# Token dispatch with weights on one Trainium2 core: later loads on the store queue, later products on VectorE alone

## The chip, the core and the metric

The kernel runs on one core of a Trainium2 chip. Three parts of the core matter here. VectorE (DVE in the profile) and ScalarE (ACT) multiply; 16 DMA engines move data between the device memory and the on-chip memory (SBUF, 128 partitions). A DMA is issued by an engine's instruction stream into a queue: those of SyncE (SP) go to queue q1 in this profile, those of ScalarE to queue q10. Both queues are served by the same 16 DMA engines.

The metric is the device time of one execution in microseconds (us), lower is better. The time before the change is the median of three runs.

## What is computed

Every token's 512 values are copied k = 2 times, each copy multiplied by its own weight. The indices are not used.

```python
# x: (16, 1024, 512) f32, expert_weights: (16, 1024, 2) f32
x_expanded = x[:, :, np.newaxis, :].repeat(k, axis=2)
weights = expert_weights[..., np.newaxis]
return (x_expanded * weights).astype(np.float32)     # (16, 1024, 2, 512)
```

So 33.5 MB are read and 67.1 MB are written, and there is one multiplication for each value written.

## The kernel before

The 16384 tokens are laid over 128 partitions, 128 tokens in each, and are worked on in six tiles: five of 24 tokens per partition and one of 8 (line 33). The text calls them tile 0 to tile 5. Each tile has these steps:

- **The load** of the tile's x into a buffer of the pool `x_pool`, which has two (line 79). L0 to L5 stand for the loads of tiles 0 to 5. A load of 24 tokens moves 6.29 MB (6144 KB, 48 KB in each partition); L5 moves a third of that. L0 is cut into six pieces (line 81), the others are one DMA each. Line 83 chooses the queue: SyncE for the last tile, ScalarE for all others.
- **The products**, in two halves of 12 tokens (`TO`), each into its own buffer `o_tile` of the pool `o_pool`, which also has two (line 98). In a half, VectorE takes tokens 0 to 3 and 6 to 9 of the 12 in two broadcast instructions of 4 tokens by 2 copies (line 121, 128 x 4096 values), and ScalarE takes tokens 4, 5, 10 and 11, one instruction for each token and copy (line 104, 128 x 512 values, eight in a half). The first half of tile 0 is different: it is made of single products on both engines (lines 104 and 110).
- **The stores**, one DMA for each half, issued on SyncE (line 137). S0a and S0b stand for the stores of tile 0, S1a and S1b for those of tile 1, and so on; tile 5 has one store, S5, of 8 tokens. A store of 12 tokens moves 6.29 MB, as much as a load of 24.

The order of issue is the program's order. `load(0)` and `load(1)` come before the loop; `load(i + 2)` comes at the end of iteration i (line 141), behind both stores of tile i. It writes the buffer that tile i was read from, so it waits until the products of tile i are done. The products of a half wait for the store that last read their `o_tile` buffer, which is the store two halves earlier, and for their tile's load. The framework derives all these waits from the buffers; each engine and each issuing stream works through its instructions in order. At the head, three small DMAs on SyncE bring the weights (lines 54 to 59).

Of the kernel before, what the change touches and what calls it, by code (L numbers as in the profile page):

```python
# [1 line left out]

# [4 lines left out]


@with_exitstack
def kernel(  # L10
    ctx: ExitStack,
    tc: tile.TileContext,
    x: bass.AP,
    expert_indices: bass.AP,
    expert_weights: bass.AP,
    out: bass.AP,
):
    nc = tc.nc

    batch, seq, hidden = x.shape  # L20
    k = expert_weights.shape[-1]
    P = nc.NUM_PARTITIONS
    ntok = batch * seq
    assert ntok % P == 0
    A_TOTAL = ntok // P

    f32 = mybir.dt.float32
    row = k * hidden
    TX = 24
    TO = 12  # L30
    CH = 4

    groups = [[24], [24], [24], [24], [24], [8]]
    assert sum(sum(g) for g in groups) == A_TOTAL

    xf = x.rearrange("b s h -> (b s) h")
    of = out.rearrange("b s k h -> (b s) (k h)")
    wf = expert_weights.rearrange("b s k -> (b s) k")

    w_pool = ctx.enter_context(tc.tile_pool(name="w_pool", bufs=1))  # L40
    x_pool = ctx.enter_context(tc.tile_pool(name="x_pool", bufs=2))
    o_pool = ctx.enter_context(tc.tile_pool(name="o_pool", bufs=2))

    w_tile = w_pool.tile([P, A_TOTAL * k], f32)

    def rows(of_all, done, T):
        return of_all[done * P : (done + T) * P, :].rearrange(
            "(p a) n -> p (a n)", a=T
        )

    T0 = sum(groups[0])
    G = len([g for g in groups[1:] if sum(g) == T0])
    head = (1 + G) * T0
    nc.sync.dma_start(out=w_tile[:, : T0 * k], in_=rows(wf, 0, T0))
    nc.sync.dma_start(
        out=w_tile[:, T0 * k : head * k].rearrange("p (g n) -> p g n", g=G),
        in_=wf[T0 * P : head * P, :].rearrange("(g p a) n -> p g (a n)", g=G, p=P),
    )
    nc.sync.dma_start(
        out=w_tile[:, head * k :], in_=rows(wf, head, A_TOTAL - head)  # L60
    )

    tiles = []
    done = 0
    for group in groups:
        T = sum(group)
        a0 = 0
        for n in group:
            tiles.append((done, T, a0, n))
            a0 += n  # L70
        done += T

    loaded = []

    def load(i):
        if i >= len(tiles):
            return
        done, T, a0, n = tiles[i]
        x_tile = x_pool.tile([P, TX * hidden], f32)
        src = rows(xf, done, T)  # L80
        step = TX // 6 if i == 0 else n

        queue = nc.sync if i == len(tiles) - 1 else nc.scalar
        for at in range(0, n, step):
            queue.dma_start(
                out=x_tile[:, at * hidden : (at + step) * hidden],
                in_=src[:, (a0 + at) * hidden : (a0 + at + step) * hidden],
            )
        loaded.append(x_tile)

    for i in range(2):
        load(i)
    for i, (done, T, a0, n) in enumerate(tiles):
        x_tile = loaded[i]
        outr = rows(of, done, T)
        for t in range(n):
            if t % TO == 0:
                o_tile = o_pool.tile([P, TO * row], f32)
            single = i == 0 and t < TO
            for kk in range(k if single or t % TO % 6 > 3 else 0):  # L100
                c = (done + a0 + t) * k + kk
                o = t % TO * row + kk * hidden
                if not single or c % 3 == 2:
                    nc.scalar.mul(  # L104
                        out=o_tile[:, o : o + hidden],
                        in_=x_tile[:, t * hidden : (t + 1) * hidden],
                        mul=w_tile[:, c : c + 1],
                    )
                    continue
                nc.vector.tensor_scalar(  # L110
                    out=o_tile[:, o : o + hidden],
                    in0=x_tile[:, t * hidden : (t + 1) * hidden],
                    scalar1=w_tile[:, c : c + 1],
                    scalar2=None,
                    op0=mybir.AluOpType.mult,
                )
            if not single and t % TO % 6 == 0:
                c = (done + a0 + t) * k
                o = t % TO * row
                m = min(CH, n - t)  # L120
                nc.vector.tensor_tensor(  # L121
                    out=o_tile[:, o : o + m * row].rearrange(
                        "p (t k h) -> p t k h", t=m, k=k
                    ),
                    in0=x_tile[:, t * hidden : (t + m) * hidden]
                    .rearrange("p (t h) -> p t h", t=m)
                    .unsqueeze(2)
                    .to_broadcast([P, m, k, hidden]),
                    in1=w_tile[:, c : c + m * k]
                    .rearrange("p (t k) -> p t k", t=m)  # L130
                    .unsqueeze(3)
                    .to_broadcast([P, m, k, hidden]),
                    op=mybir.AluOpType.mult,
                )
            if (t + 1) % TO == 0 or t + 1 == n:
                at = t // TO * TO
                nc.sync.dma_start(  # L137
                    out=outr[:, (a0 + at) * row : (a0 + t + 1) * row],
                    in_=o_tile[:, : (t + 1 - at) * row],
                )  # L140
        load(i + 2)

# [1 line left out]
_INS = ['x', 'expert_indices', 'expert_weights']  # L144
_OUTS = [((16, 1024, 2, 512), 'float32')]


# [23 lines left out]
```

## Time and profile before

| | |
|---|---|
| median of three runs | 240.34 us (240.26 to 242.69) |
| the profiled execution | 240.03 us |
| its span in the profile | 238.1 us |
| VectorE busy | 92.2 us (39%), 36 instructions |
| ScalarE busy | 54.2 us (23%), 85 instructions |
| queue q1 (SyncE: weights, stores, L5) | 69.34 MB, 67.5% of 16 DMA engines' span |
| queue q10 (ScalarE: L0 to L4) | 31.46 MB, 31.2% |

Span is the time from the first to the last event of the profile; what lies around it is 1.93 us here. The share of a queue is the time that its packets took on the DMA engines, so that 100% for both together would be 16 engines busy for the whole span. The profile also has the chain of waits that ended last, the instructions in order of time, and a table of stretches with the busy time of each engine, the share of the DMA engines and their GB/s.

Beside these views the trace holds a record of each DMA packet: its queue, start, duration and size. A load or store of 6.29 MB is 128 packets of 49152 bytes, one for each partition and eight on each DMA engine.

### The profile page before, as it was taken

The page shows a single profiled execution, that of the slowest core. Times are in us where ns is not written, and L with a number is a line of the kernel's source. Part 1 is how long each engine was busy: PE and PEld are TensorE (multiplying, and loading weights), DVE is VectorE, ACT ScalarE, POOL GpSimd, SP SyncE. Part 2 cuts the span into 40 slices and gives each one's busy share as a digit, 9 for nine tenths or more (in the row PEclk, how much of TensorE's full clock was granted, in tenths as well). Part 3 has the DMA queues.
Part 4 walks back from the last instruction along what each step waited for, and adds up shares of the span by engine and source line. Part 5 has one row for each costly group of instructions (what it writes and reads, how often), then busy time and mean ns, then how long its engine had stood idle before and what let it go on. Part 6 is the DMA issues. An engine that isn't in the chain of part 4 may idle for free.

```text
span 238.1 us, 232 instructions
## 1 busy us (share of the span) xinstructions
DVE 92.2 (39%) x36; ACT 54.2 (23%) x85; POOL 0.2 (0%) x4
## 2 busy tenths in 40 slices
DVE  0890240003919500391068085003919549019000
ACT  0841210003408000340061080003408044012000
POOL 0000000000000000000000000000000000000000
DMA  6998999999999999999999999999999999999996
GB/s 246 423 441 362 516 413 396 429 495 396 396 504 421 396 421 504 396 398 495 429 396 413 504 405 396 479 446 396 413 495 413 396 416 465 405 495 421 396 440 264
DMA packets 3986, 100.80 MB, mean 423 GB/s; under 512 B 1169, under 2 KB 1169, under 8 KB 1169
## 3 DMA queue, kind: packets, MB, share of 16 engines
q1 hardware_dynamic: 2544, 69.34, 67.5%
q10 hardware_dynamic: 1440, 31.46, 31.2%
q14 instruction: 2, 0.01, 0.0%
HBM read 33.69 MB, written 67.11 MB: 423 GB/s over the span
## 4 chain that ended last, share of the span: by engine, by line
DMA 62%; DVE 18%; another core or an unknown queue 10%; DVEq 1%; issue 0%; SPq 0%
DMA out_dram<-o_tile 50%; DVE o_tile L121 18%; DMA x_tile<-in_x_dram 12%; DVEq L166 1%; DVEq L121 0%; SPq L137 0%
## 5 line engine op out<-in xcount | busy, mean ns | idle before, releaser
L121 DVE TENSOR_TENSOR o_tile<-x_tile,w_tile 128x4096 f32<-128x4096 f32 (+1 forms) x20 | 85.6, 4316 | 121.0 <-DMA out_dram<-o_tile 85.7
L104 ACT ACTIVATE o_tile<-x_tile,w_tile 128x512 f32<-128x512 f32 x84 | 52.9, 709 | 155.0 <-DMA out_dram<-o_tile 115.8
L110 DVE TENSOR_SCALAR o_tile<-x_tile,w_tile 128x512 f32<-128x512 f32 x16 | 6.6, 483 | 6.6 <-DMA x_tile<-in_x_dram 6.6
L104 ACT ACT_TABLE_LOAD x1 | 1.3, 1283 | 6.6 <-DMA x_tile<-in_x_dram 6.6
L155 POOL MEMSET const-bfloat16-1.0<- 128x1 bf16 x1 | 0.1, 101 | 0.0
L155 POOL MEMSET const-uint8-127<- 128x1 uint8 x1 | 0.1, 101 | 0.0
L155 POOL MEMSET const-float32-0.0<- 128x1 f32 x1 | 0.1, 98 | 0.2 <-issue 0.2
L155 POOL MEMSET const-float32-1.0<- 128x1 f32 x1 | 0.1, 98 | 0.0
## 6 DMA issues: line engine op xcount, KB each, us to landing
out_dram<-o_tile SPq DMA_DIRECT2D x10, 6144.0 KB, 31.0
x_tile<-in_x_dram ACTq DMA_DIRECT2D x4, 6144.0 KB, 42.2
x_tile<-in_x_dram ACTq DMA_DIRECT2D x6, 1024.0 KB, 10.5
out_dram<-o_tile SPq DMA_DIRECT2D x1, 4096.0 KB, 17.4
x_tile<-in_x_dram SPq DMA_DIRECT2D x1, 2048.0 KB, 24.6
w_tile<-in_expert_weights_dram SPq DMA_DIRECT2D x1, 96.0 KB, 11.2
w_tile<-in_expert_weights_dram SPq DMA_DIRECT2D x1, 24.0 KB, 3.4
w_tile<-in_expert_weights_dram SPq DMA_DIRECT2D x1, 8.0 KB, 13.3
```

The source lines that it names most:

```text
L104: nc.scalar.mul(out=o_tile[:, o : o + hidden], in_=x_tile[:, t * hidden : (t + 1) * hidden], mul=w_tile[:, c : c + 1],)
L110: nc.vector.tensor_scalar(out=o_tile[:, o : o + hidden], in0=x_tile[:, t * hidden : (t + 1) * hidden], scalar1=w_tile[:, c : c + 1], scala ...
L121: nc.vector.tensor_tensor(out=o_tile[:, o : o + m * row].rearrange("p (t k h) -> p t k h", t=m, k=k), in0=x_tile[:, t * hidden : (t + m) * ...
L155: nc = _bacc.Bacc("TRN2", target_bir_lowering=False, num_devices=1)
L166: with _tile.TileContext(nc) as tc:
```

## The change

Two things change. First, every load from tile 2 on (L2 to L5) is issued on SyncE's stream, where it stands behind the second store of the tile two before it; L0 and L1 stay on ScalarE's. Second, from tile 2 on ScalarE makes no products: VectorE takes all 12 tokens of a half in three broadcast instructions of 4 tokens, at tokens 0, 4 and 8, and in tile 5 two instructions of 4 tokens. Tiles 0 and 1 are worked on as before (`shared`).

```diff
-        queue = nc.sync if i == len(tiles) - 1 else nc.scalar
+        queue = nc.sync if i >= 2 else nc.scalar
...
             single = i == 0 and t < TO
-            for kk in range(k if single or t % TO % 6 > 3 else 0):
+            shared = i < 2
+            step = 6 if shared else CH
+            for kk in range(k if single or shared and t % TO % 6 > 3 else 0):
                 c = (done + a0 + t) * k + kk
                 o = t % TO * row + kk * hidden
                 if not single or c % 3 == 2:
...
-            if not single and t % TO % 6 == 0:
+            if not single and t % TO % step == 0:
                 c = (done + a0 + t) * k
                 o = t % TO * row
                 m = min(CH, n - t)
```

## The prediction, made before the changed kernel ran

> **What bounds the kernel now.** I read the page's busy shares and DMA queues first, then the table of stretches, then the chain of waits with its order of time, and last the packet records. The page:
>
> ```profile
> DVE 92.2 (39%) x36; ACT 54.2 (23%) x85; POOL 0.2 (0%) x4
> ...
> DMA  6998999999999999999999999999999999999996
> ...
> q1 hardware_dynamic: 2544, 69.34, 67.5%
> q10 hardware_dynamic: 1440, 31.46, 31.2%
> ```
>
> The two queues together took 98.7% of 16 engines' span; neither multiplying engine is busy half of it. The table of stretches (length, busy time and count of each engine, clock, share of the DMA engines, GB/s) shows whether a stage hides a hole:
>
> ```profile
> 33.00:62.00 29.00, 4.57 (x2) 4.74 (x8) 0.00 (x0) 1.00 1.00 432
> 62.00:120.00 58.00, 21.72 (x5) 10.29 (x17) 0.00 (x0) 1.00 1.00 434
> 120.00:164.00 44.00, 17.52 (x4) 10.02 (x16) 0.00 (x0) 1.00 1.02 442
> 164.00:236.00 72.00, 32.91 (x8) 17.59 (x28) 0.00 (x0) 1.00 0.99 428
> ```
>
> There is none. By the packet records, 16 packets are in flight in every microsecond from 3 to 235; the first starts at 1.7 and the last ends at 236.9. Of 1792 packets of 49152 bytes, 1762 took exactly 1815 ns, loads and stores alike, with one queue active or two. So a 6.29 MB transfer costs 8 x 1.815 = 14.52 us of all engines, and the 100.66 MB of loads and stores cost 128 x 1.815 = 232.3 us in any order. The rest is 1.7 us at the head, 1.2 us behind the last packet, and 2.9 us more, of which some 2.1 us is small and overlapping packets in the first 20 us. The DMA engines are the bound. The chain of waits names stores and products, but each of its waits lies beside full DMA engines.
>
> **Part 1, L2, L3 and L4 from q10 to q1** (L5 is on q1 already). Nothing is added: three issues of 0.36 us leave ScalarE's stream for SyncE's, where issues of 0.33 to 0.82 us already lie between waits of up to 33.1 us. SyncE then waits for nothing new: a load needs the products that the store ahead of it has just waited for. S(i+1)a now stands behind the load's issue, and waits for its products far longer than that. The order of transfers does change. Before, a load shared the engines packet by packet with stores; now it follows S(i)b whole. What I must know is whether one queue alone keeps the engines full over the joints. The row is S3b, L5, S4a, all on q1 with q10 empty. The first engines end S3b at 192.49 us, L5 starts at 192.50; L5 ends from 197.55, S4a starts from 197.36. In the stretch from 180 to 200 the packets took 0.15 us per engine more than their bytes at 1815 ns per 49152. Three more loads with two such joints each cost 3 x 0.15 = 0.45 us at most; at the other end the loads' own excess on q10, 0.13 us from 20 to 140 us, is saved. I take +0.15, between the ends.
>
> **Part 2, products on VectorE alone.** From tile 2 on 52 ScalarE instructions go (16 in each of tiles 2, 3, 4 and 4 in tile 5) and VectorE's 13 of 4096 values and one of 2048 become 20 of 4096. The rows:
>
> ```profile
> L121 DVE TENSOR_TENSOR o_tile<-x_tile,w_tile 128x4096 f32<-128x4096 f32 x19 | 83.4, 4423 | 121.0 <-DMA out_dram<-o_tile 85.7 <-DMA x_tile<-in_x_dram 35.4
> L104 ACT ACTIVATE o_tile<-x_tile,w_tile 128x512 f32<-128x512 f32 x84 | 52.9, 709 | 155.0 <-DMA out_dram<-o_tile 115.8 <-DMA x_tile<-in_x_dram 39.1
> ```
>
> The broadcast took 4424 to 4426 ns whether or not ScalarE ran beside it. A pair with its issue took 8.83 us (179.16 to 187.99); three take 3 x 4.42 less two overlaps of some 0.08, with the issue 13.2. Each half becomes 4.4 us later; VectorE's total rises by 7 x 4.42 less 2.28 for the short one, 28.7: about 121 us of 238. None of it is on the path as long as each store is issued before its queue runs dry. That cover I now work out.
>
> **The queue after the change.** S2a starts at 120.0 and S3a at 163.5 before; by then the same transfers are done in both orders, so these times stand if no hole opens. Counting in steps of 14.52 us: S0b ends at 61.9, then L2 to 76.4, S1a to 91.0, S1b to 105.5, L3 to 120.0, S2a to 134.5, S2b to 149.0, L4 to 163.5, S3a to 178.0, S3b to 192.5, L5 to 197.4, S4a to 211.9, S4b to 226.4, S5. A landing reaches the products 1.3 us after the first engines end it (S3b 192.49, product at 193.83; S4a 211.86, product at 213.19), and 0.5 to 0.7 after the last one does; that is the row for q1 alone. Beside loads on q10 it took 2.2 us after the last end (S0b: 69.33, product at 71.53; S1a: 96.88, product at 99.07). The issue of each store, and its lead before its queue turn:
>
> - S1a at 66.3 as before (L1 is untouched), turn 76.4: lead 10. S1b: VectorE is free at 66.2, issue 75.0, turn 91.0: lead 16.
> - S2a: buffer free at 91.0 + 1.3, issue 105.5, turn 120.0: lead 14.5. S2b, S3a, S3b repeat this 14.5 us apart or so: leads 14.5.
> - S4a: 178.0 + 1.3 + 13.2 = 192.5, turn 197.4: lead 4.9. S4b: 192.5 + 1.3 + 13.2 = 207.0, turn 211.9: lead 4.9. S5: 211.9 + 1.3 + 8.8 = 222.0, turn 226.4: lead 4.4. Before, these were 9.4, 9.2 and 6.5:
>
> ```profile
> 187.99 25.07 DMA out_dram<-o_tile
> ...
> 213.19 4.43 DVE o_tile L121
> ```
>
> The short L5 and the end make the difference: between a half's buffer and its turn lie 14.5 us of another transfer and L5's 4.8, not 29, and for S5 14.5 alone. The loads land at 77.7, 121.3, 164.8 and 198.7, each some 14.5 us ahead of the products that need them.
>
> How much lead is needed? The lower bound is the first load: issued at 0.72, first packet at 1.81, so 1.1 us into idle engines. The upper bound is S3b: issued at 173.49, it started at 178.00 straight behind S3a, so 4.5 us was enough. Issues into busy engines showed their first packet after 3.9 (S0a) to 5.1 us (L3), but the engines were full meanwhile. Leads of 4.9, 4.9 and 4.4 thus cost nothing, or at the worst reading (5.1 needed) 0.2 for S4a and 0.7 for S5, 0.9 us; S4b adds none, since a late S4a moves its turn and not its products. I take 0, by S3b, the nearest row.
>
> A rule of the Trainium skill speaks against this cover: "DMA: Bandwidth & Descriptors", section "Anatomy of one DMA — SWDGE (gpsimd) path", gives a DMA some 2.0 us of fixed cost, mostly the receipt after the last byte. The 2.2 us beside q10 agree with it, the 0.5 us from S4a's last end (212.71) to its product (213.19) don't; by the rule the leads in the tail would be an estimated 1.5 us shorter.
>
> The sum: 238.1 + 0.15 + 0, so a span of some 238.3 and, with 1.93 around it, 240.2 for the profiled execution (240.03). The median stands 0.3 above that: 240.5.
>
> **The rivals.**
>
> - *Slower: the single queue stutters.* With q10 empty from 55 us on, a hole at a joint between load and store is filled by nothing. Six joints are new (S0b-L2, L2-S1a, S1b-L3, L3-S2a, S2b-L4, L4-S3a). At the 1.1 us of a start into idle engines they cost 6.6, so 247; it decides by 1% from 0.4 us a joint. Against it: S3b-L5-S4a without a hole. For it: L5's packets are of 16384 bytes, no 48 KB load has yet followed a store in one queue. 6%.
> - *Slower: the tail's stores come late.* If more lead is needed than there is, S4a and S5 leave the engines idle, each by the difference. With 5.85 us needed that is 0.95 + 1.45 = 2.4, the 1%; with 7 it is 2.1 + 2.6 = 4.7: 245. S3b's 4.5 without a hole is against it. 3%.
> - *Slower: late landings.* If stores in the tail reach the products 2.2 us behind their last end, as beside q10, and not 0.5, the leads of S4a and S5 fall by 1.7 to 3.2 and 2.7; against 4.5 needed that loses 1.3 + 1.8 = 3.1: 243.6. Every landing of the tail, where q10 was already empty before, is against it. 1%. The skill's rule above is of this kind.
> - *Faster: one kind of transfer at a time runs better.* Only the excess after 20 us, some 0.4 us, is there to win; more would need packets under 1815 ns, and the 128 packets of S2a, which ran alone, took that too. Over 1% would be 237.9 or less. 2%.
> - *It doesn't do what it says:* the framework could hold a load on SyncE for another transfer, with S(i+1)a behind it. L5's wait was 27 ns. A hold of up to one transfer passes beneath the leads of 14.5 us. No rival in time.
>
> **How the numbers follow.** Forecast, engines full throughout: 88%, 240.5, with the worst joints and leads 240.3 + 0.45 + 0.9 = 241.7; with all excess after 20 us saved 239.9. The runs of before spread from 240.26 to 242.69, so a median can stand a few tenths off: range 239.7 to 241.9. It leaves out the rivals, 12%, and little else. Within 1% (237.9 to 242.7), about what a measurement of this kernel can tell from no change: 88%; slower 6 + 3 + 1 = 10%; faster 2%.
>
> **What would show it.** Right: both queues' shares still sum to about 98.7%, with q10 at some 12.6 MB and q1 at 88.2; 1.00 in every stretch from 33 to 236; VectorE near 121 us, ScalarE near 21 us (52 x 0.63 less); S2a's, S4a's and S5's issues near 105, 192 and 222; loads that land some 15 us after the store ahead of them instead of sharing. Wrong at the joints: a share under 1 near 62, 105 and 149. Wrong in the tail: slices under 9 from 195 on. Packets that no longer take 1815 ns would overturn the whole sum.

## The result and the profile after

The changed kernel is slightly slower: 242.36 us (median of 20 runs, 240.54 to 243.23) against 240.36 us for the kernel before in the same series (20 runs, 239.88 to 243.5). The ratio is 1.0058, with a 95% interval of 1.0037 to 1.0079, or 1.4 us; it is made without disturbed runs and lies near the ratio of the means (242.10 against 240.72 without the slowest run of before). The plain medians are 2.0 apart because 14 of the 20 changed runs took 242.1 us or more and only 4 of the 20 before did. By the ratio the loss is within 1%, as forecast, but it is not zero.

The profiled execution took 241.27 us (before: 240.03), with a span of 239.1 us (238.1). So of its 1.24 us more, 1.0 lies in the span and 0.24 around it. The second part is steady: time less span was 2.14 to 2.23 us in all 20 runs of the changed kernel, and 1.88 to 1.97 in 29 runs of before. Its page answers the lines shown of before:

```profile
DVE 120.2 (50%) x42; ACT 21.5 (9%) x33; POOL 0.2 (0%) x4
...
DMA  6998999999999999999999999999999989999994
...
q1 hardware_dynamic: 2976, 88.21, 85.7%
q10 hardware_dynamic: 1008, 12.58, 12.8%
```

Both parts did what they say: VectorE has the work of ScalarE from tile 2 on, and q1 has all loads but L0 and L1. The two queues' shares sum to 98.5% (98.7% before). The table of stretches of the changed kernel (length, busy time and count of VectorE, ScalarE and GpSimd, clock, share of the DMA engines, GB/s), at the same places as before and with the first microsecond behind them:

```profile
33.00:62.00 29.00, 4.92 (x2) 4.95 (x8) 0.00 (x0) 1.00 1.00 432
62.00:120.00 58.00, 38.70 (x9) 5.08 (x9) 0.00 (x0) 1.00 1.00 432
120.00:164.00 44.00, 26.19 (x6) 0.00 (x0) 0.00 (x0) 1.00 1.02 439
164.00:236.00 72.00, 34.95 (x8) 0.00 (x0) 0.00 (x0) 1.00 1.00 430
236.00:237.00 1.00, 0.00 (x0) 0.00 (x0) 0.00 (x0) 1.00 0.16 66
```

The DMA engines are full up to 236 us, as before. There is no hole at the joints and none in front of the late stores. What is new is the last line. The table books a packet where it starts, and S5's packets of 32 KB take 1.21 us: a share of 0.16 in one microsecond is two packets that start after 236 us (2 x 1.21 / 16 = 0.15). Before, none did:

```profile
236.00:237.00 1.00, 0.00 (x0) 0.00 (x0) 0.00 (x0) 1.00 0.01 0
```

So two of the 16 engines still had a whole packet to start when others were about to end. The packet records say the same: the first engine ends its last packet at 236.04 us before and at 236.24 after, the last one at 236.90 before and 237.88 after. I call the difference of the two the **spread**: 0.86 us before, 1.64 after. Of the 0.98 us that the last packet moved, 0.78 is spread. Most of the loss in the span is not in the engines' mean work; it is in the one that comes last.

Where the spread grows can be read from each transfer's last packet on its first and its last engine (changed kernel, us, from the packet records):

```
S0b 0.49 | L2 0.49 | S1a 0.49 | S1b 0.49 | L3 0.69 | S2a 0.69 | S2b 0.69
L4 1.17 | S3a 1.17 | S3b 1.17 | L5 1.55 | S4a 1.76 | S5 1.63
```

No store from S1a to S3b changes it. L3, L4 and L5 do. (Before, the same row is 0.57 after S1b, 0.60 from S2b to S3b, 0.85 after L5, with L3 and L4 shared with stores.) L2 has three long packets too, up to 190 ns over 1815, and the spread stayed at 0.49.

### The profile page after: what moved, and what is told of

Same layout as the page of the kernel before. It is cut to its first block, busy times and chain, and to the rows that moved or that the text cites. A ratio compares the mean times of both kernels' runs of the same rounds, so it can differ in the third digit from the quotient of the medians.

```text
span 239.1 us, 173 instructions
## 1 busy us (share of the span) xinstructions
DVE 120.2 (50%) x42; ACT 21.5 (9%) x33; POOL 0.2 (0%) x4
## 4 chain that ended last, share of the span: by engine, by line
DMA 57%; DVE 24%; another core or an unknown queue 10%; DVEq 2%; issue 0%; SPq 0%
DMA out_dram<-o_tile 45%; DVE o_tile L123 24%; DMA x_tile<-in_x_dram 11%; DVEq L168 2%; DVEq L123 0%; SPq L139 0%
## 5 line engine op out<-in xcount | busy, mean ns | idle before, releaser
L123 DVE TENSOR_TENSOR o_tile<-x_tile,w_tile 128x4096 f32<-128x4096 f32 x26 | 113.6, 4421 | 96.0 <-DMA out_dram<-o_tile 61.1
L106 ACT ACTIVATE o_tile<-x_tile,w_tile 128x512 f32<-128x512 f32 x32 | 20.3, 709 | 40.0 <-DMA x_tile<-in_x_dram 38.7
```

The costliest lines, as they stand in the source:

```text
L106: nc.scalar.mul(out=o_tile[:, o : o + hidden], in_=x_tile[:, t * hidden : (t + 1) * hidden], mul=w_tile[:, c : c + 1],)
L123: nc.vector.tensor_tensor(out=o_tile[:, o : o + m * row].rearrange("p (t k h) -> p t k h", t=m, k=k), in0=x_tile[:, t * hidden : (t + m) * ...
```

## The experiments

I set up two theories. **J, joints:** a load that stands behind a store in one queue has packets over 1815 ns on some engines, the delay stays with that engine, and the slowest engine sets the end. **T, tail:** the products of VectorE alone are later and leave the last stores too little lead. All kernels were profiled and timed in turn with the kernel before on the same chip. Edits are against the kernel before where nothing else is said.

**One part of the change at a time: the queue (e1).**

```diff
-        queue = nc.sync if i == len(tiles) - 1 else nc.scalar
+        queue = nc.sync if i >= 2 else nc.scalar
```

> The loads from tile 2 on go through SyncE behind the stores; the products stay shared by both engines as before. Theory J (joints): a load that follows a store in the same queue has packets over 1815 ns on some of the 16 engines, the delays stay with the engine, and the slowest engine sets the end. Then this part alone carries the whole loss: ratio 1.004 to 1.008, the last 16 packets end over 1.3 us or more (0.85 before, 1.64 after the change), and long packets lie in L2, L3 and L4. Theory T (tail): the three short leads that VectorE alone leaves (4.6, 4.7 and 3.5 us in the profile of after) open holes. Then this kernel, whose products are as quick as before, has a ratio of 1.000.

Measured: 1.0040 (1.0012 to 1.0068). Its profiled execution took 242.17 us; the first engine ended at 236.16, the last at 239.02, a spread of 2.86. The stretches at the end of this kernel:

```profile
164.00:236.00 72.00, 24.15 (x6) 12.58 (x20) 0.00 (x0) 1.00 0.99 428
236.00:237.00 1.00, 0.00 (x0) 0.00 (x0) 0.00 (x0) 1.00 0.31 131
237.00:238.00 1.00, 0.00 (x0) 0.00 (x0) 0.00 (x0) 1.00 0.08 33
```

Four packets start after 236 and one more after 237 us, and again nothing is idle ahead of that. The products were as quick as before (S4a was issued at 189.60, 7.8 us ahead of its first packet), and the loss is there all the same. J holds, and late stores are not needed for the loss. The spread went from 0.71 at 62 us to 0.94 after L2, 1.52 after L3, 2.26 after L4 and 2.64 after L5. By the spans on record the queue alone costs 0.93 us in the mean (239.77 against 238.84 in its series), and time less span is as before, 1.89 to 1.98.

**The products alone (e2)**, with the loads on their queues of before (the changed kernel with the old line 83).

> VectorE alone makes the products from tile 2 on; the loads stay on their queues of before. Theory J: no new joints, ratio 0.999 to 1.001, last packets end over about 0.85 us. Theory T: the products of S4a, S4b and S5 are 4.4 us later than before, as in the changed kernel, so the whole loss shows here: ratio 1.004 to 1.008.

Measured: 1.0171 (1.0134 to 1.0209), 4.1 us, more than both theories expected. Neither was right: the holes are in the middle and not in the tail. The order of time of this kernel (start, length, engine, line, instruction, count, idle time before it; SPq and ACTq are the streams in which SyncE and ScalarE issue DMAs, and a row can stand for several issues):

```profile
112.48 67.70 SPq L139 DMA_DIRECT2D out_dram<-o_tile  x4
121.16 13.10 DVE L123 TENSOR_TENSOR o_tile<-x_tile,w_tile 128x4096 f32<-128x4096 f32 x3 [8.70 <-DMA out_dram<-o_tile]
134.28 0.37 ACTq L85 DMA_DIRECT2D x_tile<-in_x_dram  x1
```

and its stretches there:

```profile
178.00:182.00 4.00, 2.51 (x2) 0.00 (x0) 0.00 (x0) 1.00 0.81 344
```

S2a had the engines alone from 120.1 us; the first of them ended it at 134.62. The three broadcasts for S2b ran from 121.16 to 134.26, and S2b and L4 were both issued at 134.27 and 134.28: too late for engines that need packets at 134.62. The same happened with S3b at 179.84, S3a having ended on its first engine at 179.72. Idle time from 120 to 200 us is 0.9 us per engine. The packets took 3.6 us per engine more than their bytes at 1815 ns per 48 KB: 1.5 of it in those that started together right behind the first hole (135 to 138 us), and 2.0 in S3b's last packets and in L5's (193 to 201 us), which is 12 us and more behind the second hole. The first engine ended at 240.40 with a spread of only 0.73. Some 0.5 us of the loss lies outside the span (time less span 2.38 to 2.48 us). So the 4.4 us that VectorE alone needs longer are covered only behind loads in the same queue: there S2b's products may take until the queue has worked off L3 and S2a.

**The opposite of the change: L5 on ScalarE's queue too (e3).**

```diff
-        queue = nc.sync if i == len(tiles) - 1 else nc.scalar
+        queue = nc.scalar
```

> The other way round: L5, the one load that followed a store in one queue before the change, goes to ScalarE's queue too; products as before. Theory J: that joint's long packets (0.15 us per engine between 180 and 200 us) go, the spread at the end falls from 0.85 to some 0.6 us, time 0 to 0.5 us below before (ratio 0.998 to 1.000). Theory T: leads as before or longer, ratio 1.000.

Measured: 1.0001 (0.9974 to 1.0029), in the range of both. But the spread was 1.78 and not 0.6, in an execution of 240.96 us: all engines but one had ended by 236.63. The long packets were now four of S3b's (118 to 386 ns over 1815, from 182 to 191 us), beside L5's packets of 16 KB on the other queue. So a joint in one queue is not the only place where an engine is held up.

**A smaller dose: L4 and L5 alone on SyncE (e4).**

```diff
-        queue = nc.sync if i == len(tiles) - 1 else nc.scalar
+        queue = nc.sync if i >= 4 else nc.scalar
```

> A smaller dose: only L4 and L5 go through SyncE, L2 and L3 stay on ScalarE's queue; products as before. Theory J: one new load with joints instead of three, a third of the loss: ratio 1.001 to 1.003, spread at the end between 0.85 and 1.6 us. Theory T: 1.000.

Measured: 1.0003 (0.9967 to 1.0039), spread 0.99, profiled execution 240.24 us. The spread was as J has it; the time is too close to none to tell.

**Many joints: store and load in four pieces each, in turn (e5)** (all loads from tile 2 on through SyncE, products shared; abridged).

```diff
+                    for p in range(4):
+                        nc.sync.dma_start(out=outr[...], in_=o_tile[...])    # 3 tokens of S(i)b
+                        nc.sync.dma_start(out=x_tile[...], in_=src[...])     # a quarter of L(i+2)
```

> All loads from tile 2 on through SyncE as in e1_queue_only, products shared, but the second store of a tile and the load behind it are cut into four pieces each and issued in turn: store piece, load piece, and so on (packets of 12 KB instead of 48 KB). Theory J (the joint between store and load in one queue costs): eight joints a load instead of two, so two to four times the loss of e1_queue_only, ratio 1.008 to 1.016. Theory B (the loss comes from all 16 engines loading at once for 14.5 us, with no stores beside; in blocks of 3.6 us there is no time for it): ratio 1.000 to 1.002, last packets end over 1.0 us or less.

Measured: 1.0184 (1.0148 to 1.0221); first engine at 238.82, spread 3.94, the highest but one profiled time of all at 246.11 us. This is as J has it and not as B has it: short blocks of loads didn't help, and more joints came with more loss, here in the mean (first engine 2.8 us later) as well as in the spread. The framework issued some pieces for tile 0 in another order, and the packets are of 12 KB, so this alone doesn't separate joints from sizes.

**A lag given from outside (e6 in the kernel before, e7 in the changed one).** Three loads of 16 KB into an unused tile, on two engines each, meant to go behind S0a:

```diff
+                for j in range(3 if single else 0):
+                    nc.sync.dma_start(
+                        out=scratch[2 * j : 2 * j + 2, :], in_=xf[8 * j : 8 * j + 8, :].rearrange("(p a) h -> p (a h)", p=2)
+                    )
```

> The kernel before, with three extra loads of 16 KB into an unused tile behind S0a, each meant for two of the 16 engines, so that these get some 0.9 us more work than the others. Theory F (feedback: whichever engine is behind when a load gives way to a store has its last load packets stretched, and a lag grows with each block of loads that is not shared with stores): before has no such blocks but L5, so the lag stays what it is: ratio 1.001 to 1.005, spread at the end some 1.5 to 2 us. Theory A (long packets fall on engines at random, whatever their lag): the same.

> The changed kernel with the same three extra loads. Theory F: the extra 0.9 us of lag is multiplied at the ends of L2, L3, L4 and L5, by some 1.3 to 1.6 each: 2 us or more on top of the change's own loss, ratio to before 1.012 to 1.025, long packets of over 0.5 us on the two late engines at the end of each load. Theory A: the lag only adds, by 0.9 us at most: ratio 1.006 to 1.010.

Measured: 1.0159 (1.0109 to 1.0209) in the kernel before, 1.0152 (1.0117 to 1.0188) in the changed one. The framework put these loads at the head, at 2.2 us instead of behind S0a; ScalarE's stream was held until 14.69 us, and from 12 to 18 us the DMA engines had holes (share 0.93 and 0.89), which is part of why the first engine ended at 237.70 and 237.98 only. Beyond that, the spreads are 3.00 and 2.95. The one expected ratio that was far off is the first: with a lag, the kernel before lost as much as the changed one. In it the spread was 1.34 at 93 us and grew to 3.00 by the end, in loads that were shared with stores. F, that blocks of loads alone multiply a lag, is not borne out; a lag grows in both orders.

**The changed kernel again (e8).**

> The changed kernel once more. Theory J, as the profiles so far have it (the first engine ends at 236.0 to 236.2 us in every kernel whose queues never run dry; the time is 239.2 to 239.6 us plus the spread of the last packets, and the spread grows at loads alone, in the second and the last of a load's eight packets on an engine): whatever this execution's time, it is 239.2 to 239.6 plus its spread, and nine in ten long packets of L2, L3 and L4 stand in those two places. A median near 242.4 means a spread near 3 us in most executions. Theory T (tail): the late stores would show as engines without a packet after 197 us, and the first engine would end late, the spread staying near 0.9.

Measured: 1.0059 (1.0033 to 1.0085), median 242.38 us. The profiled execution took 241.53, with the first engine at 236.39 and a spread of 1.74: 241.53 - 1.74 = 239.8, 0.2 above the expected 239.2 to 239.6: the first engine came some 0.2 later, and time less span was 2.2 instead of 1.9. No engine was without a packet between 197 us and the first end for more than 0.01 us in the mean. Where the long packets of L2, L3 and L4 stand, counted by their place among the eight of an engine, over 25 ns long, in the profiles of e1, e4, after and this one (10 loads, 1280 packets; 40 stores of 48 KB packets, 5120 packets, beside them):

```
place in the transfer     1   2   3   4   5   6   7   8
long packets of loads     0  22   0   1   0   0   0  67
long packets of stores    2   0   0   0   0   0   0   0
```

Of 90, 89 are the second or the last: one packet behind the joint where the load takes over from the store, and the one in front of the joint where the next store takes over. In these profiles a load in full flow has one, and a store has next to none. They are 26 to 790 ns long over 1815.

In the profile of this run the engines can be told apart from 62 us on, though the records don't number them: each packet starts within 10 ns of the end of another, so the packets of one engine form a chain. (Where two engines end a packet within 10 ns of each other they can be mistaken for one another, which exchanges equal lags only.) All 16 chains can be followed to the end, and they show the sum that J speaks of. The three engines that ended last, 1.61, 1.70 and 1.85 us behind the first, had collected 1.59, 1.69 and 1.77 us over 1815 ns per 48 KB in L2 to L5, the other 13 only 0.19 to 0.66; in the stores no engine collected more than 0.05. So the delay stayed with its engine.

**More joints at whole stores: half loads, each behind one store (e9)** (four buffers of half the size), and the same on two queues as a control (e10). Shown are its main lines; the tile size and the pieces of the first loads change with them, and e10 keeps the old line 83.

```diff
-    groups = [[24], [24], [24], [24], [24], [8]]
+    groups = [[12, 12]] * 5 + [[8]]
...
-        queue = nc.sync if i == len(tiles) - 1 else nc.scalar
+        queue = nc.sync if i >= 4 else nc.scalar
...
-        load(i + 2)
+        load(i + 4)
```

> Loads of 12 tokens instead of 24 (four buffers of half the size), each behind one store, all from tile 2 on through SyncE: store, half load, store, half load. Packets of 24 KB; products shared as before. Theory J: four joints for a tile's load instead of two, so about double the loss of e1_queue_only: ratio 1.006 to 1.011, spread at the end 3 us or more. Theory B (blocks of loads alone): half as long a block, a loss like that of e1_queue_only or less, ratio 1.001 to 1.005.

> The same half loads on ScalarE's queue (the last one, of tile 5, on SyncE's, as before the change). This tells what the halves alone do. Theories J and B: 0.999 to 1.003, spread at the end about 1 us.

Measured: one queue 1.0086 (1.0055 to 1.0116), first engine 236.44, spread 2.94, execution 242.55 us. Its end:

```profile
236.00:237.00 1.00, 0.00 (x0) 0.00 (x0) 0.00 (x0) 1.00 0.23 98
237.00:238.00 1.00, 0.00 (x0) 0.00 (x0) 0.00 (x0) 1.00 0.15 66
238.00:239.00 1.00, 0.00 (x0) 0.00 (x0) 0.00 (x0) 1.00 0.08 33
```

The ratio and the spread are those that J expected. The control failed: on two queues the half loads gave 1.0433 (1.0392 to 1.0474), with engines up to 7.5 us apart at S3b and a hole of its own,

```profile
212.00:219.00 7.00, 6.76 (x2) 2.98 (x5) 0.00 (x0) 1.00 0.39 169
```

in which most engines waited for a store that others were still working off. So it doesn't tell what halves do by themselves.

Put in a row by the loads that stand behind a store on SyncE, the ratios grow with their number: none (e3) 1.0001, one (before) 1, two (e4) 1.0003, four (e1, after, after again) 1.0040, 1.0058, 1.0059, seven (e9) 1.0086, sixteen pieces (e5) 1.0184. Neighbours' intervals overlap; the ends are far apart. The last two also move smaller packets, without a control that worked, so beyond four the row is not joints alone.

## Why the prediction held, and the step that was off

- **What bounds the kernel: right.** In the profiles of before, after, after again, e1, e3, e4 and e9 the first engine ends at 236.0 to 236.4 us, and 1731 of the changed kernel's 1792 packets of 48 KB took 1815 ns.
- **The cover of the products: right, by the queue's order.** The issues forecast at 105.5, 149.0, 192.5, 207.0 and 222.0 came at 105.11, 148.80, 192.81, 207.28 and 222.96. This is the changed kernel's order of time in the tail:

```profile
179.69 13.10 DVE L123 TENSOR_TENSOR o_tile<-x_tile,w_tile 128x4096 f32<-128x4096 f32 x3 [16.33 <-DMA out_dram<-o_tile]
192.81 30.48 SPq L139 DMA_DIRECT2D out_dram<-o_tile  x3
194.15 13.10 DVE L123 TENSOR_TENSOR o_tile<-x_tile,w_tile 128x4096 f32<-128x4096 f32 x3 [1.37 <-DMA out_dram<-o_tile]
214.17 8.76 DVE L123 TENSOR_TENSOR o_tile<-x_tile,w_tile 128x4096 f32<-128x4096 f32 x2 [6.92 <-DMA out_dram<-o_tile]
```

  The leads of S4a, S4b and S5 were 4.6, 4.7 and 3.5 us (first packets at 197.44, 211.94 and 226.44) instead of 4.9, 4.9 and 4.4; S5's is shorter because the spread delays S4a's last engine. None opened a hole, so 3.5 us was enough here, and the needed lead lies between 1.1 and 3.5 rather than 4.5. The products-only kernel shows what the loss is without the cover: 4.1 us.
- **Landings: right.** S0b's products started 0.7 us after its last packet (62.48 to 63.19) and S1a's buffer was taken up 0.5 us after (91.48 to 91.98), where both took 2.2 beside q10. The 2.0 us of fixed cost that the Trainium skill gives a DMA ("DMA: Bandwidth & Descriptors", section "Anatomy of one DMA — SWDGE (gpsimd) path") is stated there for DMAs issued by GpSimd, while these are issued by SyncE and ScalarE. A wait near it was met beside the other queue only; the measured 0.5 to 0.7 decides here.
- **The joints: the mechanism was named, its term mis-sized.** I costed three more loads at up to 0.15 us *per engine* each and took +0.15 in all. Per engine that was about right: from 20 us on the packets' excess over 1815 ns per 48 KB rose from 0.28 to 0.61 us, 0.33 more, and the first engine ended 0.20 later. But the excess falls on few engines and stays there, and the end waits for the last. Dividing by 16 was the error: the term to price was the slowest engine's sum. In the profiles the spread rose by 0.78 to 0.88 us in the changed kernel and by 2.00 with the queue alone. By the ratio of 1.0058 the loss is 1.4 us; less the 0.25 that lies outside the span, the term is about 1.15 us instead of 0.15.
- **The 1.93 us around the span: carried over unchanged, and it was not.** It became 2.18 in the mean of the changed kernel's runs. The rise comes with the products: where VectorE makes them alone (after, e2, e7, e8), time less span is 2.14 to 2.48 us in every run; where both engines make them it is 1.73 to 1.98. What it consists of, no profile shows, since it lies before the first or behind the last event.
- **The rivals.** The stuttering queue (6%) had the right place, and not the mechanism or the price: no hole at a joint, but longer packets, some 1.15 us over six new joints, 0.19 each, where 1% needed 0.4. The late tail, the late landings and the faster rival did not come; the 0.4 us that the last one had to win was nearer 0.28 by the packet records.
- **The time.** 240.5 was forecast; the ratio on the 240.34 it started from gives 241.7, inside 239.7 to 241.9 near its top; the plain median of 242.36 lies above it. That the range held is partly luck: its top has 0.45 us for the joints, which cost more than twice that, and 0.9 us for late stores, which cost nothing. The median was also put 0.3 us above the profiled execution and came 1.1 above.

The profiled executions of the changed kernel, 241.27 and 241.53, are faster than its median of 242.4, and that of the queue alone, 242.17, is slower than its median of 241.75; so the spreads of single profiles don't rank the kernels. The span of every run is on record: the changed kernel's median is 240.15 us, where its profile had 239.1. With 1.2 us behind the last packet and a first end of 236.2 to 236.4, as in its profiles, such a run would have a spread of an estimated 2.6 us. That is argued; no profile of the changed kernel itself fell on such an execution.

Open: why the second and the last load packet are the long ones, and why a lag goes with longer ones. That it goes with them, the 16 chains of e8 show: in L5 the three engines that came to it 1.2 to 1.4 us behind collected 0.43 to 0.48 us, the other 13 0.05 to 0.14; in L4 the three that collected most (0.42 to 0.52) were among the four furthest behind. The test of whether the lag is the cause was spoilt at the head.

## What to carry to other kernels

When the DMA engines are full from end to end, three things moved the time in these runs: holes, longer packets, and how far apart the engines finish; so price a delay that falls on a few packets by the engine that collects them, not by its mean, and read the last microsecond of the DMA share before and after. A load placed behind stores in their queue is a cushion under which products may take longer (here 4.4 us a half without a hole), but a change between store and load in a queue can hold up some engine, and here it did. Test the two parts of such a change apart: the slower products without the queue's order cost three times what the whole change did.

## What the runs showed of the hardware

- In four profiles with loads behind stores in one queue, long load packets stand at the joints: 89 of 90 were the second or the eighth of eight, up to 790 ns over 1815. The delay stayed with its engine: in e8 the three engines that ended last had collected 1.59 to 1.77 us in loads, and none over 0.05 in stores.
- The rule of the Trainium skill that issuing from several engines only saves issue time ("DMA: Bandwidth & Descriptors", section "Issuing engines are not separate DMA queues") would, taken by itself, have the queue alone cost nothing. Moving three loads from ScalarE's queue to SyncE's cost 0.4% (0.1 to 0.7), though each issue takes under 1 us and is hidden; the order in which the engines meet loads and stores is what differs.
- A hole can cost more than its length: with the products alone, the first of two holes, 0.6 us, came with 1.5 us per engine of longer packets right behind it. The second, 1.1 us, had next to none right behind it (0.06).
